# Direct first FFN tiles, down products chained in PSUM, stores on ScalarE's queue, cond weights in steps

## The chip, the cores and the metric

The kernel runs on one core of a Trainium2 chip. The metric is the device time of one execution in microseconds. TensorE (PE in the profile) does the matmuls, VectorE (DVE), ScalarE (ACT) and GpSimd (POOL) the elementwise work, and SyncE (SP) issues most transfers. PSUM has eight banks of 512 fp32 columns for each of 128 partitions.

## The reference

One call computes two transformer blocks on a sequence of 1024 tokens of width 1024, in fp32. The change touches the two FFNs and what stands around them:

```python
# end of the first block
x = layer_norm(ALPHA * x + mix @ w_out, ln1_g, ln1_b)
gate, up = x @ w_gate, x @ w_up                  # 1024 -> 2816 each
ffn = (silu(gate) * up) @ w_down                 # 2816 -> 1024
x = layer_norm(ALPHA * x + ffn, ln2_g, ln2_b)
...
# second block: six rows of 1024 that modulate it
mod = silu(c) @ w_cond + b_cond
...
h = rmsnorm(x, g_ffn_pre) * (1 + scale_f) + shift_f
f = (silu(h @ w_gate) * (h @ w_up)) @ w_down
x = x + gate_f * rmsnorm(f, g_ffn_post)
```

## The kernel before

**Three matmuls for one.** Every fp32 operand of a large matmul is split into a high part (a cast on ScalarE, line 80 or 942) and a low part (a subtraction on VectorE or POOL, line 84 or 943). A product takes three matmuls: high x high, high x low, low x high (`mm3`, line 95).

**Seven products for eight.** Gate, up and down use the Strassen-Winograd scheme: the left matrix is cut into blocks A11 to A22, the right one into B11 to B22, sums S1 to S4 and T1 to T4 are formed of them, and seven block products p1 to p7 take the place of eight. Their results are combined afterwards: C11 = p1 + p2; with u2 = p1 + p6 and u3 = u2 + p7, C22 = u3 + p5, C21 is u3 with p4, and C12 is u2 with p5 and p3.

**Stages around the change, in order of time.** `out_proj` (line 699) multiplies the mixers' output with w_out, in eight blocks of 128 tokens; its second half ends at about 660 us. Each block is normed (`norm1`) and, two blocks later, transposed, and written as the parts of the FFN's right matrix by `SAct.put` (line 807): for blocks 0 to 3 it writes B11 and B21; for blocks 4 to 7 it writes B22 and forms T1, T2, T3. `finish` (line 843) then forms T4 = B21 - T2.

`gate_up` (line 994) walks over 11 pairs of FFN tiles. For each pair, gate and then up make their seven products (`Matrix.product`, line 936) of 12 matmuls of 512 columns. VectorE adds what comes out of PSUM in `after`; POOL multiplies silu(gate) with up (line 991), and a transfer stores the half tile to h_d (line 992, on SP). In the first FFN `cond` (line 1161) runs after pairs 1 to 6: eight loads of 512 KB, each followed by one multiply-add on VectorE (line 1170), then two matmuls with a matrix of ones. Its loads use the three "raw" buffers.

`down` (line 1031) takes the first 18 tiles of h_d in five groups, two tiles in the first and four in each other (`SIZES` 1, 2, 2, 2, 2 tiles in each of two blocks). A group has seven products of 12 or 24 matmuls; each product goes to fresh PSUM tiles (one `pmm`, one `ptr` and one wide `plg`, two buffers each) and is added on VectorE to its own accumulator in SBUF (line 1115; in the first group ScalarE copies, line 1113). In the last group `combine` (line 1045) joins the accumulators, mostly on POOL. `down_last` (line 1120) does the last four tiles as plain products, block by block of 128 tokens, and passes each block on: in the first block of the network the residual (`residual1`, line 1201), norm and modulation (`after1`), and in the second block `after2`.

**What sets the order.** The instructions of an engine, and the transfers of a queue, go in the order in which they stand in its queue. That order is found beforehand by the framework's scheduler, which goes by priorities (`soon()` raises one) and hands out the buffers of each tag; a buffer is given on when its last reader is through. Pools that are closed give their space to those opened later.

Of the kernel before, what the change touches and what calls it, by code (L numbers as in the profile page):

```python
# [9 lines left out]
F32 = mybir.dt.float32  # L10
# [11 lines left out]
S = 1024  # L22
# [16 lines left out]
def two_blocks(ctx: ExitStack, tc: tile.TileContext, a):  # L39
# [741 lines left out]
    class SAct:  # L781
# [7 lines left out]
        def __call__(self, n):  # L789
            if n not in self.t:  # L790
                if n in ("B22", "T4"):
# [5 lines left out]
            return self.t[n]  # L797

# [8 lines left out]
        def put(self, x, tb, affine=None):  # L807

            ts = slice(tb % 4 * P, (tb % 4 + 1) * P)
            halves = []  # L810
            for q in range(2):
# [16 lines left out]
            if tb < 4:  # L828
                return
            b12, b22 = halves  # L830
            b11 = [t.bitcast(F32)[:, :, ts] for t in self("B11")]
            t1, t2, t3 = self.temp(), self.temp(), self.temp()
            V.tensor_tensor(t1, b12, b11[0], op=OP.subtract)
            A.copy(t3, b22)
            G.tensor_tensor(t1, t1, b11[1], op=OP.subtract)
            V.tensor_tensor(t3, t3, b12, op=OP.subtract)
            self.part("B22", ts, b22, V)
            V.tensor_tensor(t2, b22, t1, op=OP.subtract)
            self.part("T3", ts, t3, V)
            self.part("T1", ts, t1, G)  # L840
            self.part("T2", ts, t2, V)

        def finish(self):
            (bh, bl), (th, tl) = ([t.bitcast(F32) for t in self(n)] for n in ("B21", "T2"))
            for c in range(4):
                ts = slice(c * P, (c + 1) * P)
                t = self.temp()
                G.tensor_tensor(t, bh[:, :, ts], th[:, :, ts], op=OP.subtract)
                G.tensor_tensor(t, t, bl[:, :, ts], op=OP.add)
                G.tensor_tensor(t, t, tl[:, :, ts], op=OP.subtract)  # L850
                self.part("T4", ts, t, G if c % 2 else V)
# [34 lines left out]
    def norm1(tb):  # L886
        layer_norm(acc[tb], g1, b1, G, V)
# [3 lines left out]
    x1.finish()  # L891
# [93 lines left out]
    class Up(Matrix):  # L985
        def out(self, i, l, t, o):
# [5 lines left out]
            DMA.dma_start(h_d[self.f + i][:, l * 512:(l + 1) * 512], s)  # L992

    def gate_up(act, wg, wu, nraw, npost, extra=None):
# [3 lines left out]

        def load(src):
            n_raw[0] += 1  # L1000
            shape = [P, KT, P]
            if nraw < 4 and n_raw[0] % 5 >= nraw:
                r = slot("raw", shape, F32, "raw")
            else:
                r = gp.tile(shape, F32, tag="rw", bufs=nraw, name="rw")
# [6 lines left out]
        for p in range(NFT // 2):  # L1012
            f = 2 * p

            if p == 0:
                order = ((0, 1), (1, 1), (0, 2), (1, 2), *((m, q) for m in range(2) for q in (6, 7, 5, 4, 3)))
            else:
                order = tuple((m, q) for m in range(2) for q in (1, 6, 2, 7, 5, 4, 3))
            ms = {}
            for m, q in order:  # L1020
                if m not in ms:
                    w = (wg, wu)[m]
                    ms[m] = (Gate, Up)[m]([load(w(f)), load(w(f + 1))], act, post)
                    if m == 1:
                        ms[1].gate, ms[1].f = ms[0], f
                ms[m].product(q)
            if extra is not None:
                extra(p)
        gp_done.close()

    def down(dp, wd, sizes):
# [4 lines left out]
        own = {p: dp.tile([P, 4, 512], F32, tag="ac", bufs=3, name=f"dacc{p}") for p in (1, 6, 5)}  # L1036

        def acc_of(p, c0, n):

# [5 lines left out]
        def combine(p, c0, n):  # L1045

            x = {q: acc_of(q, c0, n) for q in range(1, 8)}
            if p == 2:
# [608 lines left out]
```

## Time and profile before

| | us |
|---|---|
| median of 3 runs (2725.01 to 2730.57) | 2728.06 |
| the profiled execution | 2730.03 |
| its span, first to last instruction | 2728.3 |
| TensorE busy | 2393.6 |
| VectorE busy | 1931.6 |
| ScalarE busy | 1112.7 |
| POOL busy | 963.4 |

A busy time is the sum over an engine's instructions. TensorE's matmuls overlap in their records, so that a busy TensorE need not be at its full rate. PEclk is the granted clock of TensorE, 1.00 for 2.4 GHz and 0.50 for 1.2 GHz, as a mean over a stretch.

### The profile page before, as it was taken

To read this page: it belongs to the slowest core of one execution; us is meant where nothing else is said; L and a number is where in the kernel's file an instruction comes from. 1 tells how busy PE (TensorE), PEld (TensorE's weight loads), DVE (VectorE), ACT (ScalarE), POOL (GpSimd) and SP (SyncE) were. 2 spreads that over 40 slices of the span, in tenths; PEclk is the share of its full clock that TensorE was granted. 3 is DMA by queue.
4 is the path that set the end of the run, shared out by engine and by line. 5 is a ranking of instruction groups with operands and counts; after the bars stand their busy time and mean duration, and the time that the engine had idled before them with its cause. 6 is when DMAs were issued, how large, how long until landed. Compare 5 with 4: busy or idle time off the path is not lost. (4 is left out here: it accounts for less than half of the span.)

```text
span 2728.3 us, 32599 instructions
## 1 busy us (share of the span) xinstructions
PE 2393.6 (88%) x11488; PEld 1953.5 (72%) x11488; DVE 1931.6 (71%) x3364; ACT 1112.7 (41%) x1951; POOL 963.4 (35%) x576
## 2 busy tenths in 40 slices
PE   8889896997498999979976989898749999988987
PEld 8878775885376778857754868677537888866765
DVE  4889779559767865559979356677975555538996
ACT  4559774343232223243316344454642332325331
POOL 2220134013522222256652033435352222226684
PEclk9999998998699999989977989999969999998998
DMA  4154445425235632242043443562412222214204
GB/s 175 59 153 113 128 145 169 103 83 181 97 119 163 201 115 74 74 170 93 32 139 116 145 113 123 158 179 78 160 46 79 80 82 81 82 68 166 98 24 147
DMA packets 149792, 314.35 MB, mean 115 GB/s; under 512 B 19574, under 2 KB 65654, under 8 KB 149628
## 3 DMA queue, kind: packets, MB, share of 16 engines
q1 hardware_dynamic: 149628, 312.26, 35.4%
q8 instruction: 91, 1.49, 0.2%
q14 instruction: 73, 0.60, 0.1%
HBM read 230.39 MB, written 81.81 MB: 114 GB/s over the span
## 5 line engine op out<-in xcount | busy, mean ns | idle before, releaser
L942 ACT CAST wst<-tt 128x512 fp32r<-128x512 f32 x176 | 109.1, 621 | 309.3 <-PE plg L99 260.9
L943 POOL TENSOR_TENSOR wst<-rw,wst 128x512 fp32r<-128x512 f32 x61 | 87.1, 1429 | 345.5 <-ACT wst L942 187.8
L84 POOL TENSOR_TENSOR wl<-raw,wh 128x1024 fp32r<-128x1024 f32 (+2 forms) x28 | 68.7, 2460 | 248.6 <-ACT wh L80 220.1
L339 PE MATMUL plg<-qk,qk 128*128 128x384 f32 (+4 forms) x480 | 123.6, 372 | 20.7 <-DVE mn L352 6.8
L943 DVE TENSOR_TENSOR wst<-tt,wst 128x512 fp32r<-128x512 f32 x176 | 125.2, 712 | 15.6 <-ACT wst L942 14.7
L965 DVE TENSOR_TENSOR u<-plg,u 128x512 f32<-128x512 f32 x44 | 30.4, 690 | 129.6 <-PE plg L99 129.6
L991 POOL TENSOR_TENSOR u<-u,u 128x512 f32<-128x512 f32 x44 | 68.4, 1554 | 144.2 <-DVE u L965 78.1
L280 ACT ACTIVATE junk_a<-xi,cand 128x1024 bf16<-128x1024 f32 (+1 forms) x124 | 108.8, 878 | 14.9 <-DVE cand L269 6.7
L1458 DVE TENSOR_TENSOR_SCAN sab<-sab 128x640 f32<-128x640 f32 (+7 forms) x64 | 101.1, 1585 | 19.0 <-ACT sab L1456 18.4
L942 ACT CAST wst<-rw 128x512 fp32r<-128x512 f32 x92 | 56.7, 619 | 126.5 <-PE plg L99 88.3
L339 PEld LDWEIGHTS plg<-qk,qk 128*128 128x128 f32 x480 | 80.6, 195 | 31.1 <-DVE mn L352 11.6
L1107 PE MATMUL plg<-ws,hs 128*128 128x512 f32 x252 | 101.9, 404 | 1.1 <-DVE acc L1115 1.0
L1108 PE MATMUL plg<-ws,hs 128*128 128x512 f32 x252 | 101.0, 401 | 0.0
L1109 PE MATMUL plg<-ws,hs 128*128 128x512 f32 x252 | 100.8, 400 | 0.0
L164 PE MATMUL pmm<-wh,xh 128*128 128x256 f32 (+1 forms) x320 | 93.0, 291 | 3.1 <-DVE stgl L401 1.8
L353 ACT ACTIVATE e<-e,mn 128x128 f32<-128x128 f32 (+7 forms) x96 | 74.2, 773 | 46.0 <-DVE mn L352 42.1
L943 POOL TENSOR_TENSOR wst<-raw,wst 128x512 fp32r<-128x512 f32 x27 | 39.4, 1461 | 150.4 <-issue 85.8
L166 PE MATMUL pmm<-wh,xl 128*128 128x256 f32 (+1 forms) x320 | 91.9, 287 | 0.0
L165 PE MATMUL pmm<-wl,xh 128*128 128x256 f32 (+1 forms) x320 | 91.8, 287 | 0.0
L694 PE MATMUL pmm<-woh,mixh 128*128 128x512 f32 x192 | 80.4, 419 | 8.2 <-DVE acc L721 3.1
L1170 DVE SCALAR_TENSOR_TENSOR mod<-raw_c,sc,mod 128x1024 f32<-128x1024 f32 x42 | 61.0, 1451 | 36.7 <-DMA raw_c<-in_w_cond_dram 36.6
L84 POOL TENSOR_TENSOR hs<-hr,hs 128x1024 fp32r<-128x1024 f32 (+1 forms) x30 | 82.2, 2740 | 13.4 <-ACT hs L80 13.4
(510 smaller groups left out, 8517.5 us busy)
## 6 DMA issues: line engine op xcount, KB each, us to landing
raw_c<-in_w_cond_dram SPq DMA_DIRECT2D x48, 512.0 KB, 3.9
rw<-in_wgu_dram SPq DMA_DIRECT2D x44, 512.0 KB, 3.4
qk<-qkd SPq DMA_DIRECT2D x72, 256.0 KB, 6.1
hr<-h_d SPq DMA_DIRECT2D x36, 512.0 KB, 4.2
wr<-in_w_down_dram SPq DMA_DIRECT2D x36, 512.0 KB, 4.0
x_d<-acc SPq DMA_DIRECT2D x24, 512.0 KB, 2.8
qk<-qk2d SPq DMA_DIRECT2D x48, 256.0 KB, 4.6
h_d<-u SPq DMA_DIRECT2D x44, 256.0 KB, 2.4
```

The lines of the kernel that those rows point to most:

```text
L84: eng.tensor_tensor(lo, src, hi.bitcast(F32), op=OP.subtract)
L164: T.matmul(o, at(0, k, tb * P, P), h[:, j, :], start=(k == 0), stop=False)
L165: T.matmul(o, at(0, k, tb * P, P), l[:, j, :], start=False, stop=False)
L166: T.matmul(o, at(1, k, tb * P, P), h[:, j, :], start=False, stop=(k == KT - 1))
L280: A.activation(junk_a[:, :L], xi[self.blks[i]], AF.Sign, bias=c, accum_out=self.cnt[:, i:i + 1])
L339: T.matmul(pl[:, c, :n], q[:, isl], k2[:, c * n:(c + 1) * n], start=(j == 0), stop=last)
L942: A.copy(wh, x)
L943: (G if p in (2, 4) else V).tensor_tensor(wl, x, wh.bitcast(F32), op=OP.subtract)
L1107: T.matmul(o[:, i, :], hl[0][:, j, ts], wl[0][:, j, :], start=(j == 0), stop=False)
L1108: T.matmul(o[:, i, :], hl[0][:, j, ts], wl[1][:, j, :], start=False, stop=False)
L1109: T.matmul(o[:, i, :], hl[1][:, j, ts], wl[0][:, j, :], start=False, stop=(j == np_ - 1))
L1458: V.tensor_tensor_scan(sa[:, ::-1], sa[:, ::-1], sa[:, ::-1], 1.0, op0=OP.mult, op1=OP.bypass)
```

## The change

Six edits, in both FFNs if not said otherwise.

1. `put` writes all four blocks B11 to B22 and forms no sums. The first four FFN tiles of gate_up are computed as plain products (`direct`), tiles 0 and 1 first with tokens 0 to 511, then with the others; the new `sums` forms T1 to T4 from the stored parts after that in program order. Nine pairs are left for the seven products.
2. Stores to h_d from the nine pairs are issued by ScalarE, one product after the one that made them.
3. `cond` becomes a generator, and one step (one of eight loads with its multiply-add, or one of two halves of the matmuls) is taken after every second product of the nine pairs.
4. `down` runs its products in the order 1, 7, 6, 4, 5, 2, 3. Products 6, 5 and 3 are added in PSUM to what product 1 left there, and product 4 to product 7 (`more`; T4 of down changes its sign for that); every state is still added to an accumulator in SBUF. The combinations that are left go to VectorE.
5. The first group's tiles, all but one, are loaded to the "raw" buffers, and down_last's tiles are loaded by `down` to its own buffers. `DownPool` makes each tag a pool, in an order that is given. In the first FFN x1 is loaded into the accumulators and scaled in the first group, and `residual1` goes.
6. One addition of the layer norms goes from VectorE to POOL, for blocks 0 to 5. gate_up of the second FFN has 8 instead of 10 "post" buffers.

```diff
             for q in range(2):
...
-                if tb < 4:
-                    self.part(("B11", "B21")[q], ts, tr, V)
-                halves.append(tr)
...
+                self.part(f"B{q + 1}{tb // 4 + 1}", ts, tr, V)
+
+        def sums(self):
+            def sub(n, ts, eng, x, y):
+                t = self.temp()
+                (xh, xl), (yh, yl) = ([b.bitcast(F32)[:, :, ts] for b in self(z)] for z in (x, y))
+                eng.tensor_tensor(t, xh, yh, op=OP.subtract)
+                eng.tensor_tensor(t, t, xl, op=OP.add)
+                eng.tensor_tensor(t, t, yl, op=OP.subtract)
+                self.part(n, ts, t, eng)
+                return t
+            chunks = [slice(c * P, (c + 1) * P) for c in range(4)]
+            for ts in chunks:
+                t1 = sub("T1", ts, G, "B12", "B11")
+                sub("T3", ts, V, "B22", "B12")
...
+                V.tensor_tensor(t, xh, t1, op=OP.subtract)
+                V.tensor_tensor(t, t, xl, op=OP.add)
+                self.part("T2", ts, t, V)
+            for ts in chunks:
+                sub("T4", ts, G, "B21", "T2")
...
-        layer_norm(acc[tb], g1, b1, G, V)
+        layer_norm(acc[tb], g1, b1, G, G if tb < 6 else V)
...
-            DMA.dma_start(h_d[self.f + i][:, l * 512:(l + 1) * 512], s)
+            self.stores.append((h_d[self.f + i][:, l * 512:(l + 1) * 512], s))
...
+        def direct(f, th, g, u):
+            pg = ps_lg()
+            for n, (wh, wl) in enumerate((g, u)):
+                for k in range(KT):
+                    mm3(pg[:, n, :], wh[:, k, :], wl[:, k, :], act.at(0, k, th), act.at(1, k, th), k == 0, k == KT - 1)
+            s = post("silu")
+            with soon():
+                A.activation(s, pg[:, 0, :], AF.Silu)
+                V.tensor_tensor(s, s, pg[:, 1, :], op=OP.mult)
+            DMA.dma_start(h_d[f][:, th * 512:(th + 1) * 512], s)
...
+        wt = [load_gu(0), load_gu(1, own)]
+        for th in range(2):
+            for f in range(2):
+                direct(f, th, *wt[f])
+        for f in (2, 3):
+            wt = load_gu(f)
+            for th in range(2):
+                direct(f, th, *wt)
+        act.sums()
...
+        for p in range(2, NFT // 2):
...
+                for q in (1, 6, 2, 7, 5, 4, 3):
+                    old = list(stores)
+                    stores.clear()
+                    ms[m].product(q)
+                    for dst, src in old:
+                        A.dma_start(dst, src)
+                    if extra is not None:
+                        extra(wide)
...
-            for p, ln, rn in ((1, "A11", "B11"), (2, "A12", "B21"), (6, "S2", "T2"), (7, "S3", "T3"),
-                              (4, "A22", "T4"), (5, "S1", "T1"), (3, "S4", "B22")):
+            a = [ps_lg(), ps_lg()]
+            for p, ln, rn in ((1, "A11", "B11"), (7, "S3", "T3"), (6, "S2", "T2"), (4, "A22", "T4"),
+                              (5, "S1", "T1"), (2, "A12", "B21"), (3, "S4", "B22")):
...
+                if p in (7, 2):
+                    b = [ps_mm(512), ps_mm(512), *(ps_tr().rearrange("p a b -> p (a b)") for _ in range(2))]
+                more = p not in (1, 7, 2)
+                for c0, n in ((0, 2), (2, 2)) if p in (1, 6, 5, 3) else ((c, 1) for c in range(4)):
+                    o = a[c0 // 2] if n == 2 else b[c0][:, None, :]
...
-                        if g == 0:
+                        if g > 0:
+                            V.tensor_tensor(x, x, o, op=OP.add)
+                        elif res is not None and p not in own:
+                            V.scalar_tensor_tensor(x, x, ALPHA, o, op0=OP.mult, op1=OP.add)
+                        else:
                             A.copy(x, o)
...
+                    q = {4: 6, 2: 1}.get(p)
+                    if g == len(sizes) - 1 and q:
+                        V.tensor_tensor(x, x, acc_of(q, c0, n), op=OP.add)
+                    elif g == len(sizes) - 1 and p == 5:
+                        x7 = acc_of(7, c0, n)
+                        V.tensor_tensor(x7, x7, x, op=OP.add)
+        raws = []
+        for i in range(0, nlast, 2):
+            raws.append((load2([h_d[f + i + j][:, :] for j in range(2)], "hr"), load2([wd(f + i + j) for j in range(2)], "wr")))
+        return y, raws
...
+    def extra1(w):
+        wide[0] = w
+        n_extra[0] += 1
+        if n_extra[0] % 2 == 0:
+            next(conds, None)
```

## Rows read from the trace of the kernel before

**Rows 1.** The page: busy time, share of the span and instructions of each engine.
```profile
PE 2393.6 (88%) x11488; PEld 1953.5 (72%) x11488; DVE 1931.6 (71%) x3364; ACT 1112.7 (41%) x1951; POOL 963.4 (35%) x576
```

**Rows 2.** Stretches: length, then each engine's busy time and instructions; PEclk, DMA share, GB/s.
```profile
600.00:750.00 150.00, 98.52 (x401) 74.65 (x400) 123.74 (x223) 43.73 (x68) 61.88 (x36) 0.81 0.38 132
750.00:1050.00 300.00, 285.05 (x1191) 225.68 (x1190) 206.30 (x257) 87.28 (x147) 72.62 (x49) 0.98 0.44 142
1165.00:1220.00 55.00, 37.02 (x131) 27.22 (x130) 27.18 (x21) 25.75 (x40) 32.18 (x17) 0.81 0.48 169
1220.00:1365.00 145.00, 143.26 (x608) 113.48 (x608) 142.78 (x121) 52.49 (x53) 92.53 (x35) 1.00 0.20 72
1365.00:1410.00 45.00, 29.66 (x91) 20.36 (x90) 33.43 (x26) 8.17 (x8) 37.46 (x17) 0.71 0.36 119
1410.00:1500.00 90.00, 64.90 (x270) 50.42 (x269) 80.80 (x250) 46.50 (x73) 20.76 (x8) 0.82 0.37 132
1900.00:2050.00 150.00, 97.37 (x409) 74.48 (x408) 122.19 (x274) 80.30 (x154) 69.39 (x45) 0.81 0.31 104
2100.00:2150.00 50.00, 50.00 (x216) 40.17 (x215) 26.77 (x38) 14.76 (x26) 13.06 (x9) 1.00 0.22 79
2435.00:2490.00 55.00, 36.78 (x134) 26.53 (x133) 27.45 (x21) 26.56 (x41) 33.15 (x18) 0.84 0.47 176
...
2640.00:2680.00 40.00, 25.43 (x75) 17.31 (x74) 26.27 (x23) 8.28 (x9) 33.67 (x15) 0.70 0.35 119
```

**Rows 3.** Timeline of TensorE, out_proj: start, duration, line, operation, how many.
```profile
614.42 1.03 PE L815 MATMUL ptr<-ident,acc 128*128 128x128 f32 x8
615.21 0.47 PE L694 MATMUL pmm<-woh,mixh 128*128 128x512 f32 x1
...
658.84 0.40 PE L696 MATMUL pmm<-woh,mixl 128*128 128x512 f32 x1
```

**Rows 4.** TensorE's waits, 600 to 760: us in total, times, longest.
```profile
PE ptr L97 <- ACT wst L942: 22.3, 1, 22.3
```

**Rows 5.** Timeline of VectorE, end of out_proj.
```profile
643.98 0.64 DVE L805 TENSOR_TENSOR x1B21l<-ptr,x1B21h 128x512 fp32r<-128x512 f32 x1
...
704.23 1.74 DVE L805 TENSOR_TENSOR x1T2l<-tt,x1T2h 128x512 fp32r<-128x512 f32 x1
```

**Rows 6.** VectorE's groups, 600 to 735: busy us, mean ns, idle before.
```profile
L1170 DVE SCALAR_TENSOR_TENSOR mod<-raw_c,sc,mod 128x1024 f32<-128x1024 f32 x14 | 23.4, 1673 | 1.8 <-DMA raw_c<-in_w_cond_dram 1.8
```

**Rows 7.** Timeline of ScalarE, entry of the second FFN.
```profile
1962.32 0.59 ACT L804 CAST x3B21h<-ptr 128x512 fp32r<-128x512 f32 x1
...
2001.07 0.62 ACT L804 CAST x3T2h<-tt 128x512 fp32r<-128x512 f32 x1 [0.43 <-DVE tt L838]
```

**Rows 8.** The page: POOL's multiply in gate_up.
```profile
L991 POOL TENSOR_TENSOR u<-u,u 128x512 f32<-128x512 f32 x44 | 68.4, 1554 | 144.2 <-DVE u L965 78.1
```

**Rows 9.** VectorE's waits, 750 to 1050.
```profile
DVE mod L1170 <- DMA raw_c<-in_w_cond_dram: 34.8, 24, 3.6
```

**Rows 10.** Timeline of the SP queue, first gate_up to down.
```profile
1179.52 0.32 SPq L992 DMA_DIRECT2D h_d<-u  x1
1179.88 0.92 SPq L1065 DMA_DIRECT2D hr<-h_d  x2
```

**Rows 11.** Waits of the SP queue, 740 to 1180.
```profile
SPq L992 <- POOL u L991: 87.5, 22, 11.7
```

**Rows 12.** VectorE's groups in down, 1220 to 1350.
```profile
L1115 DVE TENSOR_TENSOR acc<-acc,plg 128x1024 f32<-128x1024 f32 x12 | 14.5, 1206 | 0.0
...
L1089 DVE TENSOR_TENSOR st<-st,hr 128x1024 f32<-128x1024 f32 x3 | 9.1, 3040 | 0.0
```

**Rows 13.** POOL's groups, 1350 to 1400.
```profile
L1049 POOL TENSOR_TENSOR acc<-acc,dacc 128x512 f32<-128x512 f32 (+1 forms) x3 | 8.0, 2664 | 6.4 <-DVE acc L1115 6.4
```

**Rows 14.** VectorE's groups in down_last, 1405 to 1500.
```profile
L870 DVE TENSOR_TENSOR acc<-acc,b 128x1024 f32<-128x1024 f32 x8 | 18.1, 2277 | 0.4 <-POOL acc L869 0.3
...
L1204 DVE SCALAR_TENSOR_TENSOR acc<-x1r,acc 128x1024 f32<-128x1024 f32 x8 | 9.7, 1216 | 1.4 <-DMA x1r<-x_d 1.3
```

More of the change, by code (lines that the diff above doesn't have):

```diff
@@ L1027, in gate_up @@
-            if extra is not None:
-                extra(p)
-        gp_done.close()
-    def down(dp, wd, sizes):
+            for m in range(2):
+                w = (wg, wu)[m]
+                ms[m] = (Gate, Up)[m]([load(w(f)), load(w(f + 1))], act, post)
+                if m == 1:
+                    ms[1].gate, ms[1].f, ms[1].stores = ms[0], f, stores
+                for q in (1, 6, 2, 7, 5, 4, 3):
+                    old = list(stores)
+                    stores.clear()
+                    ms[m].product(q)
+                    for dst, src in old:
+                        A.dma_start(dst, src)
+                    if extra is not None:
+                        extra(wide)
@@ new lines, in gate_up, with __init__, tile @@
+        flush()
+        gp_done.close()
+    DP = {"rw": (2 * D, 6), "st": (2 * 512, 6), "c": (2 * 512, 6), "ac": (4 * 512, 3)}
+    class DownPool:
+        def __init__(self, name, order):
+            self.st = ExitStack()
+            self.pl = {}
+            for tag in order:
+                self.pl[tag], done = pool(f"{name}_{tag}")
+                self.st.push(done)
+        def tile(self, shape, dtype, tag, name):
+            return self.pl[tag].tile(shape, dtype, tag=tag, bufs=DP[tag][1], name=name)
@@ L1129, in down_last @@
+        return y, raws
+    def down_last(tp, raws, y, after, between=None):
+        hs, ws = [], []
+        for n in range(2 * len(raws)):
+            for i, to in enumerate((hs, ws)):
+                r = raws[n // 2][i][:, n % 2, :]
+                if i and n < 3:
                     t = [slot("w", [P, S], F32R, "last") for _ in range(2)]
@@ L1182, in cond @@
             g = row(slot("raw", [P, D], F32, "raw_g"), a[gn])
+        for c in range(2):
+            cs = slice(c * 512, (c + 1) * 512)
+            t = wide[0]().bitcast(F32R).rearrange("p (n a) b -> p n (a b)", n=2)
+            split(t[:, 0, :], t[:, 1, :], m[:, cs])
+            o = ps_mm(512)
+            T.matmul(o, ones, t[:, 0, :], start=True, stop=False)
+            T.matmul(o, ones, t[:, 1, :], start=False, stop=True)
+            V.tensor_tensor(m[:, cs], o, b[:, cs], op=OP.add)
+            yield
+        if gn is not None:
             V.scalar_tensor_tensor(m, m, 1.0 if j in (1, 4) else 0.0, g, op0=OP.add, op1=OP.mult)
         DMA.dma_start(mod_d[j:j + 1, :], m[0:1, :])
-    def extra1(p):
-        if 1 <= p <= 6:
-            cond(p - 1)
+    wide, n_extra = [None], [0]
+    conds = chain(*(cond_steps(j) for j in range(6)))
+    def extra1(w):
[3 more added lines that the diff above has]
+            next(conds, None)
     tail = {}
@@ L1222, in two_blocks @@
     x1_done.close()
[L1223 to L1225 removed]
+    dp = DownPool("dp", ("rw", "st", "c", "ac"))
+    y1, raws1 = down(dp, lambda f: a["w_down"][f], SIZES, NLAST, x1_d)
+    dp.st.close()
     actp, act_done = pool("actp")
```

156 lines of the change are left out of this document (44 added, 112 removed).

## The prediction

> **What bounds the kernel now.** I read the page's busy times first [rows 1]: TensorE is busy 88% of the span, VectorE 71%, the others under half. An average doesn't say where TensorE is held up, so I next cut the span into stretches [rows 2] and compared each with the pace of an undisturbed one. From 2100 to 2150 TensorE did 216 matmuls of 512 columns in 50 us at full clock; with 215 that is 0.2326 us each. A transpose takes 0.10: eight begin at 614.42 and the next matmul at 615.21 [rows 3]. The loss of a stretch is its length less its matmuls at these prices; a half clock after a pause (mean PEclk 0.70 to 0.84 in the bad stretches) is then inside the loss. All counts are from [rows 2].
>
> - 600 to 750, second half of out_proj and entry of the first FFN: 317 matmuls (73.7) and 84 transposes (8.4): loss 67.9.
> - 750 to 1050, gate_up with the cond sums: 1191 (277.0): loss 23.0.
> - 1165 to 1220, gate_up to down: 131 (30.5): loss 24.5. The same in the second FFN, 2435 to 2490, 134 (31.2): loss 23.8.
> - 1365 to 1410, down to down_last: 91 (21.2): loss 23.8. Second FFN, 2640 to 2680, 75 (17.4): loss 22.6.
> - 1410 to 1500, down_last and what follows: 230 (53.5) and 40 transposes (4.0): loss 32.5.
> - 1900 to 2050, entry of the second FFN: 320 (74.4), 73 transposes and 16 short matmuls (9.2 together): loss 66.4.
>
> Together 284.5 us, all at stage borders or under the cond work. Inside down there is little: 1220 to 1365 holds 608 matmuls (141.4), a loss of 3.6, though VectorE is busy 142.8 of 145 there.
>
> **The change part by part.** Every term is a loss above, less what I think stays.
>
> *Direct tiles.* Two pairs of FFN tiles go from 168 matmuls each (2 matrices x 7 products x 12) to 192 (2 matrices x 2 tiles x 2 halves x 24). That adds 48 in each FFN, 96 x 0.2326 = **22.3 us on TensorE's path**, the one sure cost. What it buys is work that needs no block sums. Now TensorE stands still once for 22.3 us for a product with T2 [rows 4], whose parts are formed in put and finish. After the change, 96 direct matmuls (22.3 us) need only B11 and B21, whose last piece is written at 643.98 [rows 5], 15 us before the last out_proj matmul at 658.84 [rows 3]; the other 288 (67.0 us) need the puts of the last four blocks.
>
> The sums then have 67.0 us. Per 128-column chunk VectorE gets 7 operations (4 for T3, 3 for T2) and POOL 8 (4 each for T1 and T4), times four chunks: 28 and 32. VectorE's row for such a piece is 0.64 undisturbed and 1.74 beside POOL [rows 5]: 17.9 to 48.7 us. POOL's is 1.55 [rows 8]: 49.7. Both ends fit, so I cost the sums at nothing; without the cover it would be POOL's 49.7. T4 takes the place of another block when that is free; its product is the sixth of a pair, five products (60 matmuls, 14.0 us) later, against 4 x 1.55 of POOL.
>
> The SBUF page of the Trainium skill ("SBUF — State Buffer", Who interferes with whom) says that a VectorE operation with two SBUF inputs and a GpSimd operation that reads SBUF hold one port pair in turn, never both. By that rule the sums take 17.9 + 49.7 = 67.6, and the low parts of the direct weights (8 x 1.206 [rows 12]) bring 77.2, so that each entry would lose 10 more, and the sum would be 2607. The trace agrees in direction: the same operation takes 0.64 or 1.74.
>
> The first entry also loses a load: VectorE runs 14 cond steps, 23.4 us, in the middle of out_proj's norms [rows 6], and it is busy 123.7 of 150 there. They move behind the direct tiles; six of eight bias additions go to POOL. I leave 18 of the 67.9: about 6 while VectorE still sets out_proj's pace, 4 for the first direct weights, 3 where T4 meets the first pair, 5 of half clock. **Gain 49.9.** In the second entry 10 us of the loss lie before 1950 and stay; B21 is complete at 1962.3 and the last put at 2001.1 [rows 7], which fewer casts and subtractions bring to about 1990, while the 22.3 us of direct work end near 1985. So 10 + 10 + 5 + 5 = 30 of 66.4 stay. **Gain 36.4.**
>
> *cond in steps.* VectorE waits 34.8 us in 24 waits for cond weights [rows 9], and evictions that TensorE needs stand behind it in its queue. One step in two products has 24 x 0.2326 = 5.6 us for a 512 KB load, with three buffers. I leave 6 of 23.0. **Gain 17.0.** Bounds: 0 and 23.
>
> *Stores on ScalarE's queue.* The first load of down is issued at 1179.88, directly after the last store at 1179.52 [rows 10]: SP goes in order, and 22 of its stores waited 87.5 us for POOL's multiply [rows 11]. With the stores elsewhere, and the first group's tiles in buffers outside the pool, those loads pass ahead, during gate_up. A store's issue took 0.32 [rows 10]; 72 of them (9 pairs x 4 x 2 FFNs) are 23 us, hidden in ScalarE's time off (busy 14.8 of 50 [rows 2]); uncovered they would cost 23. Group 0 also sends four of seven products' evictions to VectorE in the first FFN. I leave 8 of each: the last eviction, the wide PSUM tile of the last product, and ScalarE's copies in group 0. **Gain 16.5 and 15.8.**
>
> *Down.* The number of evictions hardly changes (12 of 512 and 8 of 1024 columns for 14 and 7), and so does TensorE's work. What is new is that product 3 and the next group's product 1 share both wide PSUM tiles: half a product, 12 x 0.2326 = 2.8 us, covers an eviction of 1.21 that may stand behind a 3.04 us operation [rows 12]. Bounds for a border: 0, and 2 x (3.04 + 1.21 - 2.79) = 2.9; for eight borders 0 to 23. VectorE is nearly always busy there, so I take the lower part, **a loss of 6**. The final combinations leave POOL (about 2.7 us each [rows 13]) for VectorE, 8 short and 2 long ones against its 4 and 2 now; that is late by some 3 us and in the next term.
>
> *Down to down_last.* Now POOL works through its combinations before the low parts that down_last waits for. With those gone and the raw tiles loaded ahead, the casts and VectorE's lag stay: 11 of 23.8 and of 22.6. **Gain 12.8 and 11.6.**
>
> *Residual and norm.* VectorE loses the residual additions (9.7) and six of eight bias additions (18.1 x 6/8 = 13.6) [rows 14] in a stretch where it is busy 80.8 of 90. POOL, busy 20.8, takes six long operations, in a chain through both engines. Of the 23 us I count **9.5**, and 23 of 32.5 stay.
>
> Sum: 49.9 + 36.4 + 17.0 + 16.5 + 15.8 + 12.8 + 11.6 + 9.5 = 169.5; less 22.3 and 6: 141.2. The profiled execution took 2730.0 (span 2728.3 and 1.7 around it), so 2588.8. The median of the runs is 2.0 lower: **2587**.
>
> **The rivals.**
> 1. *The borders close better*: half of what I leave (115) goes too, 2587 - 57 = 2530. For it: direct tiles overlap with everything. Against: VectorE's chains of norms stay.
> 2. *The direct tiles start only after the puts.* The engine queues go in order, and the order is fixed beforehand; then each entry lacks its 22.3 us of filler: 2587 + 45 = 2632. For it: out_proj's loads and splits stand ahead of the FFN's in the same buffers.
> 3. *VectorE becomes the bound in down*: eight borders at 2.9 (17 more than I took) and both combinations late (10 each): 2587 + 37 = 2624. For it: 142.8 of 145 busy.
> 4. *Moving the stores changes nothing but who issues them*, because the loads wait for space that gate_up holds: both borders keep their loss, 32.3 more, 2619. The DMA page of the Trainium skill ("DMA: Bandwidth & Descriptors", Issuing engines are not separate DMA queues) says just that: all queues end on the same 16 engines, and a second one saves only issue time. The row speaks against applying it here, since a load stood 0.36 us behind a waiting store.
> 5. *Slower than before*: ScalarE inherits SP's waits. Its queue is in order, and a store that waits for POOL's multiply holds the casts behind it that TensorE needs. SP's waits were 87.5/22 = 4.0 us; 72 of them on TensorE's path are 286: 2873. It decides from 141/72 = 2.0 us each. Against: a store is issued one product (2.8 us) late, the multiply ends about 2.2 after its product (0.64 + 1.55), and casts run products ahead.
>
> **How the numbers follow.** Chances: my sum 0.48, rival 1 0.14, rival 2 0.14, rival 3 0.09, rival 4 0.08, rival 5 0.05, and 0.02 that it all cancels. The unknown costs around my sum (sums 0 to 20, cond -6 to 17, borders of down -6 to 17, ScalarE's issues 0 to 23) make it 2555 to 2625 by itself. The range reaches from rival 1 to a little above rival 2: 2530 to 2650, leaving out rival 5, the cancelling case, and the far sides of 1 and 2. About 0.2% (5 us) is what a measurement can tell from no change: faster 0.93, within it 0.02, slower 0.05.
>
> **What would show it.** TensorE's wait of 22.3 for T2 gone, and direct matmuls before the last put; loads of down issued before gate_up's last product; no wait on raw_c of some length; down's stretches as now, with waits on evictions only at product 1; POOL's low parts before down ends. The prediction is wrong if ScalarE stands waiting at its stores, or if T4 or the first direct weights leave a new pause of over 10 us at an entry.

## The result and the profile after

The changed kernel takes 2640.0 us (median of 4 runs, 2637.8 to 2641.9) against 2729.3 for the kernel before in the same job: a ratio of 0.967 (95% interval 0.966 to 0.969), 89 us less. The prediction said 2587, in a range of 2530 to 2650.

The page's busy times after, to be read beside [rows 1]:

```profile
PE 2398.2 (91%) x11584; PEld 1963.6 (74%) x11584; DVE 1889.9 (72%) x3300; ACT 1083.0 (41%) x1893; POOL 931.7 (35%) x550
```

TensorE has 96 records more, from the two direct pairs of both FFNs, in a span that is 91 us shorter (2637.0). Stretches of the changed kernel, cut at the same borders as [rows 2] (length, busy time and count of PE, PEld, DVE, ACT, POOL; PEclk, DMA share, GB/s):

```profile
592.00:767.00 175.00, 153.12 (x674) 122.49 (x674) 131.40 (x214) 45.75 (x67) 82.94 (x45) 0.93 0.40 134
767.00:1060.00 293.00, 282.52 (x1179) 223.12 (x1178) 211.50 (x264) 88.55 (x153) 75.33 (x49) 0.98 0.45 147
1120.00:1175.00 55.00, 45.49 (x168) 33.53 (x167) 36.14 (x39) 19.49 (x29) 29.80 (x17) 0.91 0.67 244
1175.00:1325.00 150.00, 146.37 (x619) 116.19 (x619) 142.11 (x122) 53.04 (x55) 89.63 (x32) 0.99 0.30 111
1325.00:1365.00 40.00, 34.88 (x134) 25.80 (x133) 33.35 (x52) 10.67 (x11) 16.09 (x6) 0.91 0.00 0
1365.00:1440.00 75.00, 59.87 (x252) 46.88 (x251) 65.78 (x216) 46.62 (x74) 31.01 (x14) 0.89 0.29 106
1825.00:1990.00 165.00, 133.09 (x580) 104.52 (x579) 128.77 (x274) 78.91 (x145) 80.19 (x46) 0.90 0.34 115
...
2350.00:2405.00 55.00, 44.73 (x168) 32.66 (x167) 31.84 (x28) 25.33 (x41) 29.39 (x17) 0.94 0.41 155
2405.00:2555.00 150.00, 147.59 (x626) 117.57 (x625) 141.51 (x122) 56.42 (x57) 90.24 (x33) 0.99 0.29 105
2555.00:2595.00 40.00, 33.50 (x129) 25.00 (x128) 31.46 (x45) 10.28 (x12) 18.68 (x7) 0.91 0.10 37
```

With the prediction's two prices (0.2326 for a matmul of 512 columns, 0.10 for a transpose) each row gives the loss that is left:

| loss of TensorE, us | before | left by the prediction | measured |
|---|---|---|---|
| first entry | 67.9 | 18 | 31.0 |
| gate_up 1 with cond | 23.0 | 6 | 18.8 |
| gate_up to down, 1 and 2 | 24.5, 23.8 | 8, 8 | 15.9, 15.9 |
| inside down, 1 and 2 | 3.6, 3.2 | 6 more in all | 6.0, 4.4 |
| down to down_last, 1 and 2 | 23.8, 22.6 | 11, 11 | 8.8, 10.0 |
| down_last 1 and after | 32.5 | 23 | 21.7 |
| second entry | 66.4 | 30 | 44.6 |

For the second FFN's gate_up and down of before, which have no row there, the same reckoning gives 2.8 (2050 to 2435, 1643 matmuls) and 3.2 (2490 to 2640, 631). That gate_up, of which no term spoke, now loses 7.1 (1990 to 2350, 1517); this is a matter of where the stretch begins. Its loss lies where the first product with T2 starts, whose wait stood in the entry's stretch before. TensorE waits 2.0 there, the ten us behind it have a half clock in part, and 2050 to 2350 loses 1.6 (1283 matmuls in 300 us). The wait, from 1990 to 2350, and the ten us:

```profile
PE ptr L99 <- DVE wst L941: 2.0, 1, 2.0
```

```profile
2020.00:2030.00 10.00, 10.00 (x38) 7.96 (x37) 8.67 (x13) 2.50 (x6) 1.32 (x1) 0.83 0.33 107
```

Where the sum of 141 was too large is seen in the table: 13 and 15 us at the entries, 13 under cond, 8 at each border into down. In the entry the wait of 22.3 for T2 [rows 4] is gone, as forecast, and another has come; TensorE's waits from 592 to 775 (us in total, times, longest):

```profile
PE ptr L817 <- DVE acc L869: 12.6, 1, 12.6
PE ptr L682 <- DVE rs_t L105: 6.4, 1, 6.4
PE ptr L97 <- ACT wst L940: 2.9, 1, 2.9
```

The 12.6 are the transposes of blocks 6 and 7, whose norm ends late. VectorE's timeline tells why (start, duration):

```profile
658.26 0.67 DVE L721 TENSOR_TENSOR acc<-acc,pmm 128x512 f32<-128x512 f32 x1
...
660.38 1.78 DVE L846 TENSOR_TENSOR tt<-x1B22h,tt 128x512 f32<-128x512 f32 x1
...
671.74 0.68 DVE L846 TENSOR_TENSOR tt<-x1B22h,tt 128x512 f32<-128x512 f32 x1
...
678.55 0.16 DVE L866 SCALAR_TENSOR_TENSOR shift<-mv,rs_y 128x1 f32<-128x1 f32 x1
```

out_proj's last addition ends at 658.9, and its block's shift (the last small step of its norm) comes 19.6 us later: between the short steps of the norms VectorE forms sums of chunks that are there already, 7.9 us in all. The same sum takes 1.78 where POOL works beside it and 0.68 where POOL is all but done; the low parts of puts and weights and the steps themselves fill the rest.

Into down, the first product now starts right behind the last of gate_up (1145.15), but product 7 only at 1151.85. ScalarE's waits there, and VectorE's share of the next 27 us:

```profile
ACT ws L80 <- POOL p L989: 7.8, 1, 7.8
```

```profile
1143.00:1170.00 27.00, 20.60 (x65) 14.32 (x65) 23.57 (x23) 9.30 (x15) 20.34 (x12) 0.81 0.71 268
```

The 7.8 are ScalarE's store of a result that POOL is still multiplying, with a cast for down's first product queued behind it. That is rival 5's mechanism, in small. Product 7 waits for something else: the cast of its T3 comes at 1151.18, as POOL ends two block sums that it begins behind its last multiplication:

```profile
1147.75 3.43 POOL L1128 TENSOR_TENSOR st<-wr 128x512 f32<-128x512 f32 x2
```

### The profile page after: what moved, and what is told of

Same layout as the page of the kernel before. It is cut to its first block, busy times and chain, and to the rows that moved or that the text cites. A ratio compares the mean times of both kernels' runs of the same rounds, so it can differ in the third digit from the quotient of the medians.

```text
span 2637.0 us, 32552 instructions
## 1 busy us (share of the span) xinstructions
PE 2398.2 (91%) x11584; PEld 1963.6 (74%) x11584; DVE 1889.9 (72%) x3300; ACT 1083.0 (41%) x1893; POOL 931.7 (35%) x550
## 5 line engine op out<-in xcount | busy, mean ns | idle before, releaser
L940 ACT CAST wst<-tt 128x512 fp32r<-128x512 f32 x144 | 89.2, 621 | 252.7 <-PE plg L99 206.8
L941 POOL TENSOR_TENSOR wst<-rw,wst 128x512 fp32r<-128x512 f32 x51 | 74.6, 1463 | 269.2 <-ACT wst L940 97.3
L97 PE MATMUL plg<-ws,hs 128*128 128x512 f32 x288 | 114.6, 398 | 5.4 <-ACT dacc L1158 2.9
L98 PE MATMUL plg<-ws,hs 128*128 128x512 f32 x288 | 113.9, 395 | 0.0
L99 PE MATMUL plg<-ws,hs 128*128 128x512 f32 x288 | 113.8, 395 | 0.0
L941 DVE TENSOR_TENSOR wst<-tt,wst 128x512 fp32r<-128x512 f32 x144 | 107.6, 749 | 8.4 <-ACT wst L940 7.8
L84 POOL TENSOR_TENSOR hs<-hr,hs 128x1024 fp32r<-128x1024 f32 (+1 forms) x30 | 69.0, 2301 | 83.6 <-ACT hs L80 70.2
L963 DVE TENSOR_TENSOR u<-plg,u 128x512 f32<-128x512 f32 x36 | 24.8, 690 | 97.4 <-PE plg L99 97.4
L940 ACT CAST wst<-rw 128x512 fp32r<-128x512 f32 x77 | 47.6, 618 | 111.1 <-PE plg L99 56.8
L989 POOL TENSOR_TENSOR u<-u,u 128x512 f32<-128x512 f32 x36 | 54.9, 1526 | 92.6 <-issue 54.9
L80 ACT CAST wh<-raw 128x1024 fp32r<-128x1024 f32 x54 | 56.4, 1047 | 72.1 <-PE pmm L98 28.2
```

Of the source, the lines that this page charges most:

```text
L84: eng.tensor_tensor(lo, src, hi.bitcast(F32), op=OP.subtract)
L97: T.matmul(out, lh, rh, start=start, stop=False, skip_group_check=more)
L98: T.matmul(out, lh, rl, start=False, stop=False, skip_group_check=more)
L99: T.matmul(out, ll, rh, start=False, stop=stop, skip_group_check=more)
L940: A.copy(wh, x)
L941: (G if p in (2, 4) else V).tensor_tensor(wl, x, wh.bitcast(F32), op=OP.subtract)
```

## The experiments

Theory: the sum was too large in three places for three reasons. At the entries, sums stand ahead of the norms that TensorE waits for. Under cond, VectorE waits for weights with evictions behind it. Into down, ScalarE stands at its stores. The rival in each place is that the wait named costs nothing, and something behind it ends last. The table gives each kernel's median, its ratio to the kernel before, and lengths from TensorE's timeline, each from the last matmul of one kind to the last of the next: *entry* from out_proj to the direct tiles, *gate_up 1* on to its last product, *down* on to its last matmul. Each length is from one execution. Between kernels that don't differ in a stage the lengths still vary: by 1.7 and 3.0 us at the entries, 5 in gate_up 1, 1.6 and 4.1 in down, and the block between the FFNs, the same in all, took 482 to 494.

| kernel | us | ratio (95%) | entry 1 | gate_up 1 | down 1 | entry 2 | down 2 |
|---|---|---|---|---|---|---|---|
| changed | 2640.0 | 0.967 (0.966, 0.969) | 111.2 | 378.8 | 196.2 | 128.3 | 194.7 |
| e1 sums late | 2628.8 | 0.965 (0.962, 0.968) | 104.9 | 377.1 | 196.4 | 124.0 | 190.6 |
| e2 and weights | 2630.2 | 0.965 (0.963, 0.968) | 101.2 | 378.0 | 195.1 | 125.9 | 190.6 |
| e3 cond ahead | 2655.1 | 0.974 (0.972, 0.976) | 110.9 | 396.1 | 196.1 | 128.6 | 193.3 |
| e4 cond 1/8 | 2628.5 | 0.964 (0.962, 0.967) | 110.9 | 367.3 | 196.2 | 128.6 | 193.2 |
| e5 stores on SP | 2643.5 | 0.970 (0.968, 0.972) | 112.2 | 383.5 | 195.1 | 128.0 | 194.7 |
| e6 POOL stores | 2643.4 | 0.970 (0.968, 0.972) | 110.8 | 377.7 | 201.6 | 127.5 | 192.6 |
| e7 and S3, T3 early | 2641.0 | 0.969 (0.967, 0.972) | 111.9 | 375.5 | 200.1 | 128.3 | 193.5 |
| e8 cond on POOL | 2641.3 | 0.969 (0.967, 0.971) | 112.5 | 379.5 | 194.8 | 127.4 | 194.0 |
| e9 group 0 direct | 2623.8 | 0.963 (0.961, 0.965) | 111.1 | 377.6 | 182.4 | 130.4 | 182.9 |
| e10 and POOL stores | 2624.2 | 0.963 (0.960, 0.965) | 111.2 | 380.5 | 181.3 | 129.0 | 183.2 |
| e11 one pair | 2652.9 | 0.974 (0.972, 0.976) | 77.9 | 421.1 | 195.8 | 84.1 | 194.1 |
| e12 e1 and e9 | 2611.2 | 0.957 (0.955, 0.958) | 106.5 | 377.3 | 188.2 | 124.6 | 183.1 |

**The entries.** e1 queues the sums behind the last put (VectorE) and behind what POOL had by then:

```diff
-        act.sums()
+        with tc.issue_after(act.behind[0]), tc.issue_after(act.behind[1]):
+            act.sums()
```

> The changed kernel with one edit: VectorE's and POOL's operations of the block sums are queued behind the last put (VectorE) and the last multiplication of the norms (POOL), in both FFNs. Theory: in the changed kernel sums of early chunks stand between the steps of the last blocks' norms (14 us from the last addition of out_proj to the last shift) and hold up the last puts; with the sums behind them the entries lose about 19 instead of 31.0 and 32 instead of 44.6, and the time goes from 2640 to about 2616. Rival: the entries are held up by the weights of the second direct tile and by the half clock, so the losses stay within 4 of what they are and the time lies between 2634 and 2644. Second rival: the sums now come too late, the first pair of products waits over 10 us for T1, T2 or T4, and the time is 2640 or more.

The 14 us of that theory count from the last block's first norm step; from the last addition it was 19.6. In e1 it is 6.3, with no sum between:

```profile
658.13 0.69 DVE L721 TENSOR_TENSOR acc<-acc,pmm 128x512 f32<-128x512 f32 x1
...
665.11 2.25 DVE L868 SCALAR_TENSOR_TENSOR shift<-mv,rs_y 128x1 f32<-128x1 f32 x1
```

The entries became 6.3 and 4.3 shorter, a half and a third of what the theory asked; the intervals of the whole times overlap with the changed kernel's. TensorE's waits from 592 to 775:

```profile
PE plg L97 <- DVE silu L1025: 6.1, 3, 3.3
PE ptr L97 <- ACT wst L942: 5.1, 1, 5.1
PE plg L99 <- DVE wl L84: 2.7, 1, 2.7
```

The wait of 12.6 is gone. What came instead are the second tile's weights (2.7), the direct tiles' own evictions (6.1), and the first product with T2 (5.1 where it was 2.9): the sums are now late by that much. e2 also takes the first FFN's gate weights of the second tile out of the ring whose buffers the two rows of the norm hold, and in both FFNs it traces them ahead of the first tile's:

```diff
-        wt = [load_gu(0), load_gu(1, own)]
+        g1w = load_split(wg(1), [P, KT, P], alloc=own if nraw > 4 else slot)
+        wt = [load_gu(0), (g1w, load_split(wu(1), [P, KT, P], alloc=own))]
```

> As the run with the late sums, and in the first FFN the gate weights of the second direct tile get buffers of their own instead of the ring that the two rows of the first norm hold until its end. Theory: these weights were split only at 682 to 685, behind the norm, and TensorE's order (half 0 of tile 0, then half 0 of tile 1) had nothing to do before; with them early, another 5 to 10 us of the first entry's loss go, and the second entry is as in the run with the late sums. Rival: the late puts alone end the wait, so nothing is gained beyond the late sums (within 3 us).

3.7 us less in the first entry, 1.9 more in the second; nothing that the whole time can tell. In the second entry e1 shortens the waits for the last puts and leaves the 6.7 for B11's cast. e1, 1860 to 1950, and then the first of these waits in the changed kernel, where the 6.7 is the same:

```profile
PE ptr L817 <- DVE x3B12l L808: 7.1, 2, 3.7
PE plg L97 <- ACT x3B11h L807: 6.7, 1, 6.7
```

```profile
PE ptr L817 <- DVE x3B12l L808: 11.3, 2, 7.1
```

e11 asks what the second direct pair is worth:

```diff
-        for f in (2, 3):
-            wt = load_gu(f)
-            for th in range(2):
-                direct(f, th, *wt)
-        for p in range(2, NFT // 2):
+        for p in range(1, NFT // 2):
```

> The changed kernel with one pair of tiles computed directly in each FFN instead of two: 24 matmuls less in each (11.2 us in both together), and half the work to cover the sums with. Theory: POOL's 49.7 us of sums need more than the 33.5 us of the last three quarters of two direct pairs' halves that are left, so the first pairs of products wait 10 us or more in each FFN, and the time is 2645 or more. Rival: the sums are early enough (they begin before the puts end), and the second pair is mostly cost: 2628 to 2634.

The second pair's 24 extra matmuls per FFN cost 5.6 and buy more. Entry and gate_up 1 together are 499.0 with one pair (490.0 with two), so the loss is 14.6 larger. Waits from 592 to 775:

```profile
PE ptr L817 <- DVE acc L869: 21.0, 1, 21.0
PE ptr L97 <- ACT wst L940: 6.7, 1, 6.7
```

The wait grew to 21.0, but not by the sums: between out_proj's last addition and the last shift VectorE's are 7.9 us as before. With one pair less the cond steps begin earlier, at 666.6 instead of 716.8, and five of their multiply-adds (8.8 us) now stand between the norms' steps as well, so that the shift comes 26.8 us after the addition. e11, VectorE:

```profile
678.43 3.29 DVE L1210 SCALAR_TENSOR_TENSOR mod<-raw_c,sc,mod 128x1024 f32<-128x1024 f32 x1 [0.52 <-DMA raw_c<-in_w_cond_dram]
681.64 0.15 DVE L866 SCALAR_TENSOR_TENSOR shift<-mv,rs_y 128x1 f32<-128x1 f32 x1
```

So e11 changes two things in the first FFN. In the second, which has no cond steps, entry and gate_up together are 0.2 longer (490.0 for 489.8) with 5.6 us less of matmuls: there the second pair gives back what it costs and hardly more.

**cond.** e3 traces each load a step ahead and keeps the multiply-add behind the evictions traced before it:

```diff
+            r = ahead.pop() if ahead else cond_load(j, k)
...
+                ahead.append(cond_load(j + (k == KT - 1), (k + 1) % KT))
...
+            tc.keep_in_program_order(s)
```

> The changed kernel with one edit in the cond steps: the load of step k+1 is traced one step ahead of its use, and each multiply-add is kept behind the evictions traced before it on VectorE. Theory: VectorE's 36 us of waits for cond weights hold up evictions that TensorE needs, and cost it most of the 18.8 lost from gate_up's start to 1060; with the loads ahead these waits fall under 10 us, the loss goes to about 7, and the time from 2640 to about 2628. Rival: the waits are idle time that costs TensorE nothing, or the loads are late for another reason (SP's queue standing at the loads of FFN weights); the loss stays at 15 or more and the time between 2634 and 2644.

e4 leaves seven of each sum's eight loads and multiply-adds out:

```diff
+            if k:
+                yield
+                continue
```

> A bound: the changed kernel with one of the eight loads and multiply-adds of each cond sum kept and seven left out (42 of 48; the modulation is then not the reference's). Theory: the cond work is what costs TensorE in this stretch beyond the second gate_up's pace (7.1 in 360 us); the loss of 18.8 goes to 7 or less and the time to about 2628. Rival: the loss there comes from the sums of the entry, the first pair and the half clock after it; the loss stays at 13 or more and the time at 2634 or more.

e8 gives the loads another queue:

```diff
-            DMA.dma_start(r, a["w_cond_2"][k * P:(k + 1) * P, j * D:(j + 1) * D])
+            G.dma_start(r, a["w_cond_2"][k * P:(k + 1) * P, j * D:(j + 1) * D])
```

> The changed kernel with one edit: the loads of the cond weights are issued on POOL's queue, not SP's. Theory: in the changed kernel SP waits about 108 us in 48 cond loads for one of three buffers, and 63 us at FFN weights that stand for the tiles which the cond sums took from their ring; each holds up the other's loads, VectorE then waits 36 us for cond weights with evictions behind it, and this is most of the 11.3 that the cond work costs; with two queues the stretch loses 5 to 10 us less, 2640 to about 2632. Rival: the cost is VectorE's own time (42 multiply-adds of 1.7), so nothing is gained (2636 to 2644), or POOL's queue, standing at a load, holds up its multiplications and the time rises over 2644.

e4 gives the price of the 42 steps that it leaves out: 11.5 us of gate_up 1. VectorE waits 36.1 us in 24 waits for cond weights in the changed kernel, as before [rows 9]; in e3 it has no such wait, and gate_up 1 became 17.3 longer. From 800 to 1120, SP's longest waits and ScalarE's for FFN weights in e3:

```profile
SPq L1209 <- DVE mod L1222: 184.6, 30, 24.0
```

```profile
ACT wst L940 <- DMA rw<-in_wgu_dram: 17.4, 4, 7.1
```

SP now stands at cond loads whose buffers VectorE frees late, and FFN weights stand behind them. In e8 the waits for those buffers went to POOL (65 us in 21), VectorE still waited 30.2 us in 20, and the time stayed. So the theory falls in the form it had: its wait can go and TensorE lose more. But e3 put another queue's wait in its place, and the price of VectorE's waits alone isn't isolated. TensorE's own waits show a part: from 767 to 1060 it waits 4.7 us for evictions on VectorE in the changed kernel, and not at all for them in e4:

```profile
PE plg L97 <- DVE u L963: 3.1, 3, 1.3
PE plg L97 <- DVE p L966: 1.6, 2, 1.2
```

Whether VectorE's own time, its waits or the traffic make these evictions late, and what the rest of the 11.5 is, stays open.

**The stores and the border into down.** e5 undoes the move of the stores alone:

```diff
-                        A.dma_start(dst, src)
+                        DMA.dma_start(dst, src)
```

> One part undone: the changed kernel with the stores of the products' results back on SP's queue. Theory (the prediction's): SP's loads of FFN weights and of down's first tiles stand behind stores that wait for POOL's multiplications; both borders from gate_up to down get back what they gained (24.5 and 23.8 in place of 15.9), gate_up 2 too loses a little, and the time goes from 2640 to 2656 or more. Rival (the loads wait for space anyway, and ScalarE no longer stands at its stores): no loss, 2630 to 2644.

e6 moves the three of the last pair that POOL multiplies to POOL's queue:

```diff
+            if t is not None and self.f == NFT - 2:
+                G.dma_start(h_d[self.f + i][:, l * 512:(l + 1) * 512], s)
```

> The changed kernel with one edit: of the last pair of each gate_up, the three results that POOL multiplies are stored from POOL's own queue, right behind the multiplication, and not from ScalarE's. Theory: ScalarE stood 7.8 us at such a store before it could cast the tiles of down's first products; without this the product 7 of group 0 no longer waits for it, and each border loses about 10 instead of 15.9: 2640 to about 2628. Rival: POOL's own order (block sums S3 and T3 of group 0 behind its last multiplications) ends last, so the wait only changes its name: each border within 2 us of 15.9, and 2634 to 2644.

e7 has that, and two sums of group 0 ahead:

```diff
+                    if g == 0 and n in ("S3", "T3"):
+                        t = slot("w", [P, 1, 512], F32, "st0")
+                        with soon():
+                            eng.tensor_tensor(t, x, z, op=op)
```

> As the run with POOL's own stores, and the sums S3 and T3 of group 0 are formed ahead of POOL's last multiplications, in buffers of the ring of split tiles; the second weight tile of group 0 has a buffer there too, so that its load needs no space that gate_up holds. Theory: both causes together are the border; each loses 8 or less instead of 15.9, and the time goes from 2640 to 2624 or less. Rival: what ends last is the eviction of the last wide products and the half clock after it; each border keeps over 12, and the time stays over 2632.

With all stores of the products back on SP neither border is longer and the time can't be told from the changed kernel's (intervals 0.968 to 0.972 and 0.966 to 0.969). gate_up 1 was 4.7 longer in the one profile, about what it varies by; whether the stores did that isn't shown. e5's SP queue ahead of down:

```profile
1119.28 0.32 SPq L1101 DMA_DIRECT2D hr<-h_d  x1
...
1142.64 0.32 SPq L1058 DMA_DIRECT2D h_d<-u  x1
...
1146.50 0.32 SPq L1058 DMA_DIRECT2D h_d<-p  x1
1146.87 0.96 SPq L1101 DMA_DIRECT2D wr<-in_w_down_dram  x1
```

The first group's load passes the stores on the same queue, so the store's queue isn't what held it. Its buffer outside down's pool is the likely reason, but no run took that back alone. The group's one tile with a buffer in the pool (last row) does stand behind the stores here. In the changed kernel it is issued 13 us earlier, and neither border is shorter for it:

```profile
1133.53 0.54 SPq L1101 DMA_DIRECT2D wr<-in_w_down_dram  x1
```

In e6 and e7 ScalarE no longer stands at a store; in e7 product 7 starts at 1144.48 instead of 1151.85, or 1.3 instead of 6.5 us after gate_up's last matmul. Down is 4 to 5 us longer all the same in the first FFN and 1 to 2 shorter in the second. e7's timeline (the end of a row: idle before, and what ended it) and its 27 us from 1143:

```profile
1144.48 0.73 PE L97 MATMUL pmm<-ws,hs 128*128 128x512 f32 x2
...
1153.80 0.50 PE L97 MATMUL pmm<-ws,hs 128*128 128x512 f32 x1 [2.62 <-ACT ws L80]
1156.46 0.79 PE L97 MATMUL pmm<-ws,hs 128*128 128x512 f32 x1 [2.17 <-DVE acc L1164]
```

```profile
1143.00:1170.00 27.00, 16.18 (x46) 9.57 (x44) 24.07 (x23) 7.26 (x13) 15.11 (x9) 0.79 0.61 227
```

The 5 us gained are lost in the products behind, where VectorE is busy 24.07 of 27 and TensorE waits for its sums (a cast stands behind one), low parts and evictions. Group 0 has 19.5 us of matmuls (84) and asks for 8 sums, 14 low parts and its evictions. So e9 multiplies it directly, e10 with POOL's stores too:

```diff
+            if g == 0:
...
+                for tb in range(NB):
+                    o = ps_lg()
+                    for j in range(2):
+                        for dh in range(2):
+                            mm3(o[:, dh, :], hl[j][0][:, ts], hl[j][1][:, ts], wl[j][0][:, ds], wl[j][1][:, ds], j == 0, j == 1)
...
+                            V.scalar_tensor_tensor(y[tb], y[tb], ALPHA, of, op0=OP.mult, op1=OP.add)
...
+                continue
```

> The changed kernel with one edit: the first group of down (two tiles of 128 rows) is multiplied directly, 96 matmuls in place of 84 and no block sums, into the four quarters that the later groups add to. Theory: what ends last at the border from gate_up to down is VectorE's and POOL's work for group 0 (8 block sums and 14 low parts for 19.5 us of matmuls, VectorE busy 23.6 of 27); with 8 splits of whole tiles left, each border loses about 8 instead of 15.9, at 2.8 us more of matmuls: 2640 to about 2630. Rival: the border is ScalarE standing at its stores before it can cast down's tiles, so the wait stays and the time is 2640 to 2650.

> As the run with the direct first group, and the last pair's results that POOL multiplies are stored from POOL's queue. Theory: both waits stood one behind the other, and only with both away does the border close: 5 us or more below the run with the direct group alone (about 2624). Rival: the stores matter as little here as with the block sums, where they changed nothing that can be measured: within 4 us of the direct group alone.

Down became 13.8 and 11.8 shorter with 12 matmuls (2.8) more in each. TensorE's waits of e9 from 1120 to 1180, all of them, and its 27 us:

```profile
PE plg L98 <- DVE ws L84: 1.1, 2, 0.6
PE plg L97 <- DVE p L966: 0.9, 1, 0.9
PE plg L97 <- DVE u L963: 0.9, 1, 0.9
PE plg L97 <- DVE u L971: 0.5, 1, 0.5
```

```profile
1143.00:1170.00 27.00, 25.15 (x103) 18.88 (x104) 16.25 (x13) 4.20 (x4) 17.03 (x7) 1.00 0.87 335
```

103 matmuls where the changed kernel did 65, at a granted clock of 1.00 instead of 0.81. The edit takes work from three engines at once (ScalarE 9.30 to 4.20, POOL 20.34 to 17.03), so that it shows group 0's sums, splits and evictions to be the border's cost, but not whose part of them. In the first FFN the rows name two engines: POOL's sums ahead of product 7 in the changed kernel, and VectorE, busy 24.07 of 27, behind it in e7. In the second, where ScalarE copies all of the group's results, VectorE is less full, and the edit gains nearly as much. The 27 us behind gate_up there, in the changed kernel and then in e9:

```profile
2374.00:2401.00 27.00, 19.89 (x65) 13.45 (x63) 20.36 (x15) 15.77 (x28) 19.50 (x11) 0.87 0.76 291
```

```profile
2371.00:2398.00 27.00, 24.61 (x101) 18.45 (x101) 8.89 (x7) 12.00 (x14) 14.01 (x6) 1.00 0.93 362
```

e10 can't be told from e9, so the last pair's stores on ScalarE cost nothing that can be measured here either.

**Together.** e12 is e1 and e9 in one.

> The two edits that gained, together: block sums of the entries behind the last put, and the first group of down multiplied directly. Theory: they act in stretches 370 us apart and add up: 0.9649/0.9674 and 0.963/0.9674 give a ratio of about 0.9605 to the kernel before, some 2619 us, 20 below the changed kernel; the entries about 105 and 124 from the end of out_proj to the last direct matmul (111 and 128 in the changed kernel), down 182 and 183 (196 and 195). Rival: what one gains is lost again in the block between the two FFNs, whose length went up and down by several us in these runs; then 2624 to 2630.

2611.2 us: 29 below the changed kernel and 12.6 below e9 alone, with intervals apart from both. The gains add up: 29 for the 11 and 16 of e1 and e9, and e1's edit, whose own gain the intervals could not tell, is told by e12 against e9. The rival's 2624 did not come. The block between the FFNs was 489.2 in e12's profile, no longer than in e1 (490.1) and e9 (491.5), but 7 to 9 us longer in all three than in the changed kernel's (482.5); whether the edits or the execution do that isn't shown. The profile is of an execution of 2618.7 us; its down 1 was 188.2, not 182: TensorE waits 2.9 us there for an accumulator on VectorE, and the granted clock from 1143 to 1170 is 0.92.

## Why the prediction was right, and where it was too large

The direction, the direct tiles that begin before the last puts, and the terms behind down hold; the sum of 141 came out as 89 to 91. That 2640 lies in the range is in part luck: it lies above the 2555 to 2625 that the prediction gave its own sum, and the room above came from rival 2 (2632), whose late direct tiles did not come. Three terms were too large at once instead.

*Direct tiles.* The cost, 22.3 for 96 matmuls, is exact. The gain was 36.9 and 21.8 for 49.9 and 36.4. The step that failed is "Both ends fit, so I cost the sums at nothing". They do fit in the 67 us, but nothing made them wait for that time: VectorE takes them in a queue fixed beforehand, between the norms' steps. e1 shows 6.3 and 4.3 of the miss. The prediction left 4 for "the first direct weights"; the second tile's are another 3.7 in e2. The remainder, some 3 in the first entry and 10 in the second, was not taken away by any run; the second entry's waits for put's casts speak for the chain of norms there. The Trainium skill ("SBUF — State Buffer", Who interferes with whom) says that such VectorE and GpSimd operations hold one port pair in turn; by that rule each entry was to lose 10 more. The trace agrees in direction (1.78 beside POOL, 0.68 without, for the same sum), but a share of the misses came from what stood in the queue, as e1 shows. The prediction's two rows in [rows 5] are not that comparison: POOL was busy beside the 0.64 too, but that operation reads one input from PSUM (ptr), and the one of 1.74 reads both from SBUF. POOL in the kernel before:

```profile
643.59 2.61 POOL L869 TENSOR_TENSOR acc<-acc,ln1g 128x1024 f32<-128x1024 f32 x1 [10.13 <-ACT acc L868]
```

The sums' lower bound hardly moves by it (0.68 for 0.64). The alternative of POOL's whole 49.7 in the open did not come.

*cond in steps.* 4.2 gained for 17.0. The step that failed is "evictions that TensorE needs stand behind it in its queue", as the measure of what the 34.8 us cost: the waits stayed (36.1), and without them e3 was slower. 42 of the 48 cond steps together cost 11.5 (e4), of which 4.7 are seen as TensorE's waits for evictions.

*Stores on ScalarE's queue.* The term was 32.3, the borders gave 16.5, and e5 shows that the queue gave none of it that can be measured. The step that failed is reading [rows 10]: that a load is issued 0.36 us behind a store that had waited doesn't show that the store held it up. By e5 the queue doesn't hold the group's first tiles; their buffers are what is left. Rival 4 was right about the queue, and about the space as far as e5's rows go, but wrong that the borders would then gain nothing, since the change gave the first group other buffers as well. That part was not undone alone, so its share in the 16.5 is argued from e5, not shown. The Trainium skill ("DMA: Bandwidth & Descriptors", Issuing engines are not separate DMA queues), that a second issuing engine saves only issue time, agrees with e5: 53.4 + 32.4 + 17.2 = 103 us of waits at stores on SP from 800 to 1150, and no longer border. What is left of the border was neither the wide tile nor ScalarE's copies alone, as the prediction put it, but the sums, splits and evictions of group 0 (e9), with VectorE the next to hold it up once POOL's two sums are early (e7).

*Down* lost 3.6 more for the 6 set, *down to down_last* kept 8.8 and 10.0 for 11, the *tail* 21.7 for 23: these sizes hold, and no run undid one of them alone. For down the size is luck, as the evictions at product 1 that it was priced by hardly came. From 1175 to 1325 one of TensorE's three waits is for one, and in the second FFN none is:

```profile
PE pmm L97 <- ACT ws L80: 2.2, 2, 1.8
PE plg L97 <- DVE acc L1156: 1.4, 1, 1.4
```

The 4.3 that the second gate_up loses are the entry's: its first wait for T2 fell into that stretch (in the first FFN, likewise, the 2.9 of that wait are in gate_up's 18.8). With them the second entry's gain is 17.5, not 21.8.

Of the rivals, VectorE as the bound in down (3) came true in the first FFN's group 0 alone, and ScalarE at its stores (5) as a wait of 7.8 whose removal gained nothing. So a sign that the prediction named for being wrong, ScalarE standing at its stores, did come, but not as what set the time. The new pause of over 10 us at an entry came too (12.6), from the norms and not from T4 or the first weights.

## What to carry to other kernels

Work that is given "time to spare" still goes wherever the queue's order puts it: ask ahead of which waiting instruction it lands, and pin it behind the last one that matters. A long wait in a queue is no price; before it enters a sum, name what TensorE misses because of it, or take it away on the chip and look, and then check that no other queue took the wait over. At a border between stages count the sums, splits and evictions of the first group against its matmuls: where they don't fit, do that group without block sums.

## What the runs showed of the hardware

- A store's issue mostly takes 0.33 us on ScalarE's queue and 0.32 on SP's; on POOL's, in e6 and e7, the instruction is there for 0.58 to 0.71. e7:

```profile
1138.31 0.71 POOL L991 DMA_DIRECT2D h_d<-u  x1 [0.31 <-POOL u L989]
```

- With the waits at the border closed (the longest of them 2.9 us) the granted clock rose too: 27 us there had 0.81 in the changed kernel and 1.00 in e9, in the second FFN 0.87 and 1.00, so that part of each border's loss was half clock, not waiting.
- A sum of two SBUF tiles on VectorE took 0.68 alone and up to 1.78 beside POOL; one with an input from PSUM took 0.64 beside POOL.
